# Interleaving two arrays: each DMA queue carries loads and stores in a fixed order

## The chip, the core and the metric

The kernel runs on one core of a Trainium2 chip. The core's compute engines work in an on-chip memory of 128 partitions, and DMA engines, 16 of them, move data between that memory and the chip's main memory (HBM). The metric is the device time of one execution in microseconds (us). Before the change the median of three runs is 314.26 us (314.11 to 314.35).

## The reference

The reference takes two float32 arrays x and y of shape 32 x 256 x 1024 and interleaves them along the last axis:

```python
def reference(x, y):
    batch, seq, dim = x.shape
    result = np.zeros((batch, seq, dim * 2), dtype=np.float32)
    result[..., 0::2] = x
    result[..., 1::2] = y
    return result.astype(np.float32)
```

Each input has 33.55 MB, the output 67.11 MB. Every byte is read once and written once, 134.22 MB in all, and nothing is computed: the output is x and y woven together element by element.

## The kernel before

**Tiles.** Each input is taken as one flat run and cut into n = 8 tiles of 128 partitions by W = 8192 values, 4 MiB each, 32 KiB to a partition. A tile of x and a tile of y make 8 MiB of output. In a tile, partition p holds 8192 neighbouring values of the flat input, so its output is 16384 neighbouring values; the output is handled in two halves of 8192 values a partition (h = 0 and 1), 4 MiB each.

**Buffers.** There are two buffers for x (`xt`), two for y (`yt`), used by even and odd tiles in turn, and two for the output (`ot`), where `ot[0]` always takes half 0 of a tile and `ot[1]` half 1.

**Weaving.** VectorE (DVE in the profile) does all of it, four copies a tile: for each half, one copy of 4096 values of x a partition into the even places of `ot[h]` (L67), and one of y into the odd places (L70). Each copy counts up the semaphore `woven`, so that tile k has been woven when `woven` is 4k + 4. Before the first copy of a half VectorE waits until the tile's x has landed, and, from the second tile on, until the store that last read `ot[h]` has landed (`osem[h]`). Before the first y copy it waits for y.

**Who issues what.** DMAs are issued from two engines, SP (its queue is q1 in the profile) and ScalarE (ACT, queue q10). Each queue starts its transfers in the order of issue, and an engine that waits for a semaphore holds back everything behind it in its own program.

- SP issues the loads: the left half of x's first tile (L45), then all of y's first tile (L55), then for each tile x (L52) and y (L55). From the third tile on, x waits until the third copy of the tile two before (which frees that `xt`), and y until the fourth.
- ScalarE issues the right half of x's first tile (L46), and then all stores (L76): for each tile and half, wait until both copies of the half are done, then store. The very first store, half 0 of tile 0, is cut into a quarter (8 KiB a partition) and the rest (24 KiB).

So apart from the first half tile, one queue carries loads and the other stores. The first DMA of each of the two engines is moved ahead of the barrier that opens the program (in `tile_interleave_kernel`), so that it is issued at once.

**The end.** ScalarE waits for all stores of half 0 and clears the semaphores (L83); SP waits for all stores of half 1 (L84).

The functions that the change touches, and what calls them:

Of the kernel before, what the change touches and what calls it, by code (L numbers as in the profile page):

```python
# [3 lines left out]


def _interleave(nc, x, y, out):
    P = 128
    W = 8192
    H = W // 2  # L10

    total = 1
    for s in x.shape:
        total *= s
    n = total // (P * W)
    assert n * P * W == total
# [8 lines left out]
    ot = [nc.alloc_sbuf_tensor(f"ot{b}", [P, W], fp32).ap() for b in (0, 1)]  # L25

    xsem = [nc.alloc_semaphore(f"xsem{b}") for b in (0, 1)]
    hsem = nc.alloc_semaphore("hsem")
    ysem = [nc.alloc_semaphore(f"ysem{b}") for b in (0, 1)]
    woven = nc.alloc_semaphore("woven")  # L30
    osem = [nc.alloc_semaphore(f"osem{b}") for b in (0, 1)]
# [24 lines left out]

    for k in range(n):
        b = k % 2
        for h in (0, 1):
            c = slice(h * H, (h + 1) * H)  # L60
            if h == 0:
                nc.vector.wait_ge(xsem[b], 16 * (k // 2 + 1))
            elif k == 0:
                nc.vector.wait_ge(hsem, 16)
            if k:
                nc.vector.wait_ge(osem[h], stored(k, h))
            nc.vector.tensor_copy(out=ot[h][:, 0::2], in_=xt[b][:, c]).then_inc(woven, 1)  # L67
            if h == 0:
                nc.vector.wait_ge(ysem[b], 16 * (k // 2 + 1))
            nc.vector.tensor_copy(out=ot[h][:, 1::2], in_=yt[b][:, c]).then_inc(woven, 1)  # L70

    for k in range(n):
        for h in (0, 1):
            nc.scalar.wait_ge(woven, 4 * k + 2 * h + 2)
            for c in parts(k, h):
                nc.scalar.dma_start(  # L76
                    out=os_[k][:, h * W : (h + 1) * W][:, c], in_=ot[h][:, c]
                ).then_inc(osem[h], 16)

    nc.scalar.wait_ge(osem[0], stored(n, 0))  # L80
    used = sorted(s.num for s in [*xsem, hsem, *ysem, woven, osem[0]])
    assert used == list(range(used[0], used[-1] + 1)), used
    nc.scalar.sem_clear(range(used[0], used[-1] + 1))  # L83
    nc.sync.nop(nofuse=True).wait_op(osem[1], stored(n, 1), "sem-ge").then_inc(  # L84
        osem[1], -stored(n, 1)
    )


def kernel(tc, x, y, out):
    nc = tc.nc  # L90
    tc.close()
    tc.compile()

    _interleave(nc, x, y, out)

    blocks = nc.main_func.blocks
    for engine in (mybir.EngineType.SP, mybir.EngineType.Activation):
        opening = blocks[0].instructions
# [14 lines left out]
        opening.insert(gate, moved)  # L113
        at.instructions = body
        blocks[0].instructions = opening


# [1 line left out]
_INS = ['x', 'y']  # L119
_OUTS = [((32, 256, 2048), 'float32')]  # L120


# [23 lines left out]
```

## Time and profile before

| | |
|---|---|
| median of three runs | 314.26 us |
| profiled execution, device time | 314.21 us |
| its span (first to last instruction) | 312.9 us |
| moved through HBM | 67.11 MB read, 67.11 MB written, 429 GB/s over the span |
| VectorE busy | 71.9 us, 32 copies of 2.29 us |
| VectorE waiting for stores to free an output buffer | 206.3 us in 14 waits |
| 4 MiB loads of x, y, median from issue to landing | 24.4 us, 41.5 us |
| 4 MiB stores, median from issue to landing | 34.1 us |

How to read it: the span is what one profiled execution shows between its first and its last instruction; its device time is 1.3 us longer. The page gives the busy share of the DMA engines in 40 equal slices, where a 9 means 90% or more, and for each queue the number of packets, the megabytes and the time that they took as a share of 16 engines over the span. A packet is what one engine moves in one go: here one partition's row of a transfer, or the small one that reports its end. The waits list says which engine stood idle for what: total, number of times, longest. The view by windows gives, for chosen stretches of the span, what was busy and how many GB/s were moved.

### The profile page before, as it was taken

How to read it: one execution, taken by the hardware profiler on the slowest of the kernel's cores; microseconds unless marked ns; L12 is line 12 of the kernel's file. 1: busy time of each engine (PE TensorE's matmuls, PEld its weight loads, DVE VectorE, ACT ScalarE, POOL GpSimd, SP SyncE). 2: the span in 40 equal slices, each digit the busy share in tenths (PEclk: the TensorE clock that was granted, in tenths of full speed). 3: DMA queues.
4: the chain of work that ended last, by engine and by line, in shares of the span. 5: the costliest groups of instructions: out<-in, count | busy, mean ns of one | idle time of the engine just before them, and what ended most of it. 6: DMA issues, size and time to landing. Idle time of an engine off the chain costs nothing.

```text
span 312.9 us, 114 instructions
## 1 busy us (share of the span) xinstructions
DVE 71.9 (23%) x32; POOL 0.2 (0%) x4
## 2 busy tenths in 40 slices
DVE  0216000501305023050230503205032050415400
POOL 0000000000000000000000000000000000000000
DMA  8999999999999999999999999999999999999998
GB/s 344 461 406 431 436 402 431 440 465 406 448 423 431 440 406 465 402 469 402 469 402 465 406 457 415 436 436 419 452 402 469 402 469 402 469 402 461 411 444 360
DMA packets 4896, 134.22 MB, mean 429 GB/s; under 512 B 544, under 2 KB 544, under 8 KB 544
## 3 DMA queue, kind: packets, MB, share of 16 engines
q10 hardware_dynamic: 2592, 69.21, 51.3%
q1 hardware_dynamic: 2304, 65.01, 48.5%
HBM read 67.11 MB, written 67.11 MB: 429 GB/s over the span
## 4 chain that ended last, share of the span: by engine, by line
DMA 82%; DVE 12%; issue 0%
DMA out_dram<-ot 76%; DMA yt<-in_y_dram 7%; DVE ot L70 6%; DVE ot L67 6%
## 5 line engine op out<-in xcount | busy, mean ns | idle before, releaser
L67 DVE COPY ot<-xt 128x4096 f32<-128x4096 f32 x16 | 36.7, 2295 | 218.0 <-DMA out_dram<-ot 206.3
L70 DVE COPY ot<-yt 128x4096 f32<-128x4096 f32 x16 | 36.6, 2288 | 8.0 <-DMA yt<-in_y_dram 8.0
L130 POOL MEMSET const-uint8-127<- 128x1 uint8 x1 | 0.1, 102 | 0.0
L130 POOL MEMSET const-bfloat16-1.0<- 128x1 bf16 x1 | 0.1, 101 | 0.0
L130 POOL MEMSET const-float32-0.0<- 128x1 f32 x1 | 0.1, 98 | 0.2 <-issue 0.2
L130 POOL MEMSET const-float32-1.0<- 128x1 f32 x1 | 0.1, 98 | 0.0
## 6 DMA issues: line engine op xcount, KB each, us to landing
out_dram<-ot ACTq DMA_DIRECT2D x15, 4096.0 KB, 34.1
yt<-in_y_dram SPq DMA_DIRECT2D x8, 4096.0 KB, 41.5
xt<-in_x_dram SPq DMA_DIRECT2D x7, 4096.0 KB, 24.4
out_dram<-ot ACTq DMA_DIRECT2D x1, 3072.0 KB, 32.8
xt<-in_x_dram SPq DMA_DIRECT2D x1, 2048.0 KB, 11.7
xt<-in_x_dram ACTq DMA_DIRECT2D x1, 2048.0 KB, 13.4
out_dram<-ot ACTq DMA_DIRECT2D x1, 1024.0 KB, 16.1
```

Source lines behind the costliest of these rows:

```text
L67: nc.vector.tensor_copy(out=ot[h][:, 0::2], in_=xt[b][:, c]).then_inc(woven, 1)
L70: nc.vector.tensor_copy(out=ot[h][:, 1::2], in_=yt[b][:, c]).then_inc(woven, 1)
L130: nc = _bacc.Bacc("TRN2", target_bir_lowering=False, num_devices=1)
```

## The change

Both queues now carry loads and stores. SP has x and half 0 of the output, ScalarE has y and half 1. Each issues in a fixed order.

- At the start: SP loads the left halves of x's and y's first tiles, then x's second tile; ScalarE loads the right halves, then y's second tile. A new semaphore `gsem` reports y's right half.
- Then for each tile k: SP waits for the first two copies, stores half 0, waits for the third copy, and loads x of tile k + 2 into the buffer just freed. ScalarE waits for all four copies, stores half 1, and loads y of tile k + 2.
- The first store is no longer cut in two.
- The last tile is not woven into `ot`. Its half 0 goes into the `xt` buffer, and its half 1 into the `yt` buffer, that tile 6 has left free. VectorE waits for its own count `woven` to reach 28 before it writes there, and not for `osem`.
- The copies of VectorE, their order and their shapes stay as they are, apart from that destination. In the changed file the copies are lines L78 and L83, the stores L57 and the loads of tiles 2 to 7 L63.
- `osem` is allocated in another place, so that the range that ScalarE clears at the end is still one run of numbers.

```diff
-    Q = W // 4
+    def woven_in(k, h):
+        if k == n - 1:
+            return (xt if h == 0 else yt)[(k + 1) % 2]
+        return ot[h]
 
-    def parts(k, h):
-        return [slice(0, W)] if k or h else [slice(0, Q), slice(Q, W)]
+    lo, hi = slice(0, H), slice(H, W)
+    nc.sync.dma_start(out=xt[0][:, lo], in_=xs[0][:, lo]).then_inc(xsem[0], 16)
+    nc.scalar.dma_start(out=xt[0][:, hi], in_=xs[0][:, hi]).then_inc(hsem, 16)
+    nc.sync.dma_start(out=yt[0][:, lo], in_=ys[0][:, lo]).then_inc(ysem[0], 16)
+    nc.scalar.dma_start(out=yt[0][:, hi], in_=ys[0][:, hi]).then_inc(gsem, 16)
+    nc.sync.dma_start(out=xt[1], in_=xs[1]).then_inc(xsem[1], 16)
+    nc.scalar.dma_start(out=yt[1], in_=ys[1]).then_inc(ysem[1], 16)
 
-    def stored(k, h):
-        return 16 * sum(len(parts(j, h)) for j in range(k))
-
-    nc.sync.dma_start(out=xt[0][:, :H], in_=xs[0][:, :H]).then_inc(xsem[0], 16)
-    nc.scalar.dma_start(out=xt[0][:, H:], in_=xs[0][:, H:]).then_inc(hsem, 16)
     for k in range(n):
         b = k % 2
-        if k >= 2:
-            nc.sync.wait_ge(woven, 4 * (k - 2) + 3)
-        if k:
-            nc.sync.dma_start(out=xt[b], in_=xs[k]).then_inc(xsem[b], 16)
-        if k >= 2:
-            nc.sync.wait_ge(woven, 4 * (k - 2) + 4)
-        nc.sync.dma_start(out=yt[b], in_=ys[k]).then_inc(ysem[b], 16)
+        for h, (eng, t, src, sem) in enumerate(
+            ((nc.sync, xt, xs, xsem), (nc.scalar, yt, ys, ysem))
+        ):
+            eng.wait_ge(woven, 4 * k + 2 * h + 2)
+            eng.dma_start(
+                out=os_[k][:, h * W : (h + 1) * W], in_=woven_in(k, h)
+            ).then_inc(osem[h], 16)
+            if k + 2 < n:
+                if h == 0:
+                    eng.wait_ge(woven, 4 * k + 3)
+                eng.dma_start(out=t[b], in_=src[k + 2]).then_inc(sem[b], 16)
...
-            if k:
-                nc.vector.wait_ge(osem[h], stored(k, h))
-            nc.vector.tensor_copy(out=ot[h][:, 0::2], in_=xt[b][:, c]).then_inc(woven, 1)
+            if 0 < k < n - 1:
+                nc.vector.wait_ge(osem[h], 16 * k)
+            if k == n - 1 and h == 0:
+                nc.vector.wait_ge(woven, 4 * k)
+            dst = woven_in(k, h)
+            nc.vector.tensor_copy(out=dst[:, 0::2], in_=xt[b][:, c]).then_inc(woven, 1)
             if h == 0:
                 nc.vector.wait_ge(ysem[b], 16 * (k // 2 + 1))
-            nc.vector.tensor_copy(out=ot[h][:, 1::2], in_=yt[b][:, c]).then_inc(woven, 1)
+            elif k == 0:
+                nc.vector.wait_ge(gsem, 16)
+            nc.vector.tensor_copy(out=dst[:, 1::2], in_=yt[b][:, c]).then_inc(woven, 1)
 
-    for k in range(n):
-        for h in (0, 1):
-            nc.scalar.wait_ge(woven, 4 * k + 2 * h + 2)
-            for c in parts(k, h):
-                nc.scalar.dma_start(
-                    out=os_[k][:, h * W : (h + 1) * W][:, c], in_=ot[h][:, c]
-                ).then_inc(osem[h], 16)
...
-    nc.scalar.wait_ge(osem[0], stored(n, 0))
+    nc.scalar.wait_ge(osem[0], 16 * n)
```

More of the change, by code (lines that the diff above doesn't have):

```diff
@@ L25, in _interleave @@
     ot = [nc.alloc_sbuf_tensor(f"ot{b}", [P, W], fp32).ap() for b in (0, 1)]
+    osem = [nc.alloc_semaphore(f"osem{b}") for b in (1, 0)][::-1]
     xsem = [nc.alloc_semaphore(f"xsem{b}") for b in (0, 1)]
     hsem = nc.alloc_semaphore("hsem")
+    gsem = nc.alloc_semaphore("gsem")
     ysem = [nc.alloc_semaphore(f"ysem{b}") for b in (0, 1)]
     woven = nc.alloc_semaphore("woven")
-    osem = [nc.alloc_semaphore(f"osem{b}") for b in (0, 1)]
     xs = [rows(x, P * W, k) for k in range(n)]
@@ L64, in _interleave @@
                 nc.vector.wait_ge(hsem, 16)
[L65 to L67 removed]
+            if 0 < k < n - 1:
[4 more added lines that the diff above has]
+            nc.vector.tensor_copy(out=dst[:, 0::2], in_=xt[b][:, c]).then_inc(woven, 1)
             if h == 0:
                 nc.vector.wait_ge(ysem[b], 16 * (k // 2 + 1))
[L70 to L81 removed]
+            elif k == 0:
+                nc.vector.wait_ge(gsem, 16)
+            nc.vector.tensor_copy(out=dst[:, 1::2], in_=yt[b][:, c]).then_inc(woven, 1)
+    nc.scalar.wait_ge(osem[0], 16 * n)
+    used = sorted(s.num for s in [*xsem, hsem, gsem, *ysem, woven, osem[0]])
     assert used == list(range(used[0], used[-1] + 1)), used
     nc.scalar.sem_clear(range(used[0], used[-1] + 1))
[L84 to L85 removed]
+    nc.sync.nop(nofuse=True).wait_op(osem[1], 16 * n, "sem-ge").then_inc(
+        osem[1], -16 * n
     )
```

## The prediction, made before the changed kernel ran

> **What bounds the kernel now.** I read the page first: its two DMA lines and the queues.
>
> ```profile
> span 312.9 us, 114 instructions
> DVE 71.9 (23%) x32; POOL 0.2 (0%) x4
> DMA  8999999999999999999999999999999999999998
> DMA packets 4896, 134.22 MB, mean 429 GB/s; under 512 B 544, under 2 KB 544, under 8 KB 544
> q10 hardware_dynamic: 2592, 69.21, 51.3%
> q1 hardware_dynamic: 2304, 65.01, 48.5%
> ```
>
> The two queues (q1 is issued by SP, q10 by ScalarE) together occupy 16 DMA engines for 99.8% of the span, while VectorE is busy for 23%. The question is whether that busy time is full speed. The view by windows, cut where transfers land, answers it (window, its length, VectorE and POOL busy, clock, DMA share, GB/s):
>
> ```profile
> 2.00:22.00 20.00, 2.30 (x1) 0.00 (x0) 1.00 1.01 433
> ...
> 26.00:32.60 6.60, 2.72 (x2) 0.00 (x0) 1.00 0.98 392
> ...
> 193.07:231.80 38.73, 9.01 (x5) 0.00 (x0) 1.00 1.00 433
> ...
> 283.84:293.52 9.68, 4.50 (x3) 0.00 (x0) 1.00 1.00 433
> 293.52:303.20 9.68, 4.49 (x2) 0.00 (x0) 1.00 1.00 433
> ```
>
> The first row holds loads alone, first on two queues and then on one. The third is a whole tile in the steady part, loads on one queue and stores on the other. The last two hold stores alone, on one queue. All show 433 GB/s, so neither direction nor the number of queues moves the rate. One row stands out: 392 GB/s around the first stores.
>
> The trace's records of single packets say what the rate is made of. A 32 KiB packet (one partition's row) takes 1.213 us and the next on the same engine starts 1.210 us after it, load or store. 16 KiB steps take 0.607, 24 KiB 0.908, 8 KiB 0.305, and a completion packet 0.006. A 4 MiB transfer puts 8 rows on each engine: 8 x 1.210 + 0.006 = 9.69, and the trace has 9.68. I weighed every packet at these steps and compared the sum with the time that passed. From 1.38 us, when the first packet starts, only four stretches lose anything: 0.89 us up to 11.7 (the first 16 KiB packets take 1.0 to 1.5 instead of 0.61), 0.47 between 27.4 and 32.6 (loads beside the first 8 KiB stores take 1.25 to 1.59 instead of 1.213), 0.05 around 40 (the first 24 KiB stores) and 0.21 in the last 9.7 us (engines end 0.33 apart). The sum: 1.38 + 309.85 of packets + 1.62 lost = 312.85, against a span of 312.88.
>
> The waits show that VectorE is never late, and the timeline shows the end:
>
> ```profile
> DVE ot L67 <- DMA out_dram<-ot: 206.3, 14, 28.9
> ...
> 288.42 9.96 ACTq L76 DMA_DIRECT2D out_dram<-ot  x2
> 293.51 2.30 DVE L67 COPY ot<-xt 128x4096 f32<-128x4096 f32 x1 [5.12 <-DMA out_dram<-ot]
> ```
>
> VectorE waits 206.3 us for output buffers. The last store is issued at 298.0, while its predecessor runs until 303.2; there is no gap to close at the end. The chain of waits puts 82% on DMA and 12% on copies, but those copies lie beside other transfers: the windows around them still move 433 GB/s.
>
> The profiled execution took 314.21 us, 1.33 more than its span; the median of the three runs is 314.26.
>
> **The change, part by part.**
>
> *Packets.* Before: 4 MiB loads 7 of x and 8 of y, 15 such stores, two 2 MiB halves of x, and a first store cut into 1 and 3 MiB: 34 transfers. After: 14 loads and 16 stores of 4 MiB, four halves of 2 MiB: again 34. The first store becomes whole (1.210 instead of 0.305 + 0.908 a row: -0.02 for 8 rows), y's first tile becomes halves (2 x 0.607 instead of 1.210: +0.03). Sum 0.0. SP and ScalarE issue 17 each (before 16 and 18) at 0.33 to 0.48 us each on the issuing queue, always with earlier transfers still in the ring.
>
> *Order in the rings.* Each ring now holds load, store, load, store. If both have packets, they take turns row by row (the trace shows q1, q10, q1, q10 from 3.2 us on), so two 4 MiB transfers, one of each ring, take 2 x 9.68 = 19.36. Loads of tiles 0 and 1 (16.8 MB) end at 1.38 + 0.89 + 4 x 9.68 = 41.0; the stores of tile 0 end at 60.4, the loads of tile 2 at 79.7, the stores of tile 1 at 99.1, and so on: 38.72 a tile, as now. For most of the time both rings go in the same direction; the windows price that at 433 either way.
>
> *The waits.* A ring runs dry only if its next transfer comes late. Tile k's copies start when tile k-1's stores have landed; four copies take 2.30 + 3 x 2.21 = 8.9 us. SP's store of tile k is issued after two of them (4.5 us), its x load after three, ScalarE's store and y load after four. Meanwhile the rings hold the loads of tile k+1, 19.36 us of work. The cover left is 19.36 - 8.9 = 10.4 us for ScalarE and 14.9 for SP, so I cost these waits at nothing. Behind SP's wait for the store is queued its x load of tile k+2, which waits with it; it goes into the ring behind that store and is not wanted before the store has left it, 19.36 us later. If the cover were gone, up to 8.9 us a tile would show.
>
> *The last tile.* The loads of tile 7 land when tile 6's stores start. Woven into the freed xt and yt buffers, it needs no output buffer: 8.9 us of copies under 19.36 us of tile 6's stores. The added wait on VectorE's own count costs one copy's drain, under 0.1 us (2.29 busy against 2.21 from start to start), and is covered. Without the spare buffers, the copies would wait for tile 6's stores with nothing behind them: 4.5 us of idle rings.
>
> *The first stores.* This is the one term that the trace cannot price. They now follow loads in both rings, at 40 instead of 28 us, in 32 KiB rows. The loss was 0.47 beside 8 KiB rows; the nearest row in size (24 KiB) lost 0.05, but came after stores had been running. The bounds are 0 and 0.94 (both rings lose it); I take 0.25, between the two rows. That is 0.25 - 0.52 = -0.27.
>
> *The end.* Both rings now end near each other. ScalarE's clearing of semaphores (0.063 us at 303.2 before) can fall behind the last landing: 0 to +0.06; I take +0.03. The spread of the engines, 0.33, stays.
>
> *A rule that speaks against.* In the windows and packets, a load row that follows a store row on the same engine starts as promptly as any other, 1.210 us after it. The Trainium skill (HBM Reference, Latency) gives 0.2 us for an access to HBM on average and 2 us under high load; if each of the 7 turns from stores back to loads exposed one, an estimate by that page would be +1.4 to +14 us. By the rows the turns cost 0, and the trace does not agree for turns between two rings; turns inside a ring it does not show.
>
> The sum: 314.21 + 0.0 - 0.27 + 0.03 = 313.97, which I round to **314.0**.
>
> **The rivals.**
>
> *A. Every turn costs (slower).* In the changed kernel both rings turn from loads to stores and back. The rings turn 8 times to stores and 7 times to loads; before, the kernel had one such turn, at 27.4. If the 0.47 lost there is the price of starting stores after a stretch of loads, and not of the first stores alone, 7 more of them cost 3.3 us: 317.3. If turning back to loads costs as much as the start of the first loads (about 0.72 us of too long packets per engine), 7 x 0.72 = 5.0 comes on top: 322.3. At a tenth to a half of the first price it is 314.3 to 315.6. For it: the loss is real, and sits exactly at the first change of direction. Against it: in the steady part each engine changes direction at every row without losing anything, and at 277.8, where loads run out and only stores are left, no packet is late. It decides from 0.63 / 14 = 0.045 us a turn. Chance 0.24, most of it between 315.0 and 317.3.
>
> *B. The first loss goes and something of the edges with it (faster).* All that can go is 1.62 us; the start (0.89) and the spread (0.21) come from packets that the change leaves alone. Losing the whole 0.47 and 0.05 gives 314.21 - 0.52 = 313.7, still short of 0.2%. Only with a shorter start or end does it get to 313.4. Chance 0.17.
>
> *C. The change does not do what it says: a ring runs dry after all*, for example because one ring falls behind and a store is issued after its ring has emptied. The other ring then uses the engines alone at 433 GB/s (rows 283.84 and 293.52), so nothing is lost until both are empty, more than 10.4 us too late. At the last tile it would cost 4.5 us: 318.5. Chance 0.03.
>
> **How the numbers follow.** A measurement of this kernel can tell about 0.2% from no change, 0.63 us: 313.63 to 314.89. The forecast, no measurable change with the time between 313.65 and 314.85, has 0.56. Slower is A and C, 0.27; faster is B, 0.17. The forecast's own range is 313.7 to 314.7 (the bounds 0 and 0.94 of the first stores, with 0.06 at the end). The stated range, 313.5 to 316.0, takes in most of B and the cheaper half of A; outside it lie the dearer half of A (0.12), C (0.03) and about 0.04 of B.
>
> **What the profile of the changed kernel would show.** Right: both queues near 50%, and a DMA line of nines; windows of 19.36 us that hold loads only and then stores only, each at 433 GB/s; VectorE waiting about 30 us a tile for the output, and at tile 7 for the loads of x instead, near 272 us; the last store of each ring issued more than 10 us before its ring runs empty; a tile every 38.72 us. Wrong for the waits: slices under 9 in the DMA line, or both rings idle. A would show as a tile period above 38.72 with packets longer than 1.213 us at each turn, and as windows under 433 GB/s around it. The first stores are right if the stretch around 41 us loses less than 0.47. The prediction fails if a turn inside a ring has a price that turns between rings do not have.

## The result, and the profile after

The changed kernel takes 317.39 us (median of five runs, 316.78 to 317.93), the kernel before 314.22 us (five runs, 314.11 to 314.35). The ratio is 1.0102, with a 95% interval of 1.0087 to 1.0117: 3.2 us slower. The prediction was 314.0, between 313.5 and 316.0. The profiled execution took 317.93 us, with a span of 316.6 (before 314.21 and 312.9). In five of the kernels below single runs lie more than 1.5% above the kernel's fastest; the ratios leave those out, and a median that holds them is marked with a star.

The page of the changed kernel, its first lines:

```profile
span 316.6 us, 114 instructions
...
DVE 71.4 (23%) x32; POOL 0.2 (0%) x4
...
DMA  8999999999999999999999999999999999999995
...
DMA packets 4896, 134.22 MB, mean 424 GB/s; under 512 B 544, under 2 KB 544, under 8 KB 544
...
q10 hardware_dynamic: 2448, 67.11, 49.6%
q1 hardware_dynamic: 2448, 67.11, 49.3%
```

The packets and bytes are the same as before, evenly split now. The DMA line has its nines as before: no slice shows empty queues. Only its last digit fell, from 8 to 5. Yet the span is 3.7 us longer, so the engines were busy for longer with the same bytes, and at the end some of them had nothing left to do. The view by windows (window, its length, VectorE and POOL busy, clock, DMA share, GB/s) shows both:

```profile
2.00:22.00 20.00, 2.60 (x2) 0.00 (x0) 1.00 1.01 433
36.32:46.00 9.68, 0.00 (x0) 0.00 (x0) 1.00 0.95 383
43.00:60.00 17.00, 0.00 (x0) 0.00 (x0) 1.00 1.00 434
82.00:99.00 17.00, 0.00 (x0) 0.00 (x0) 1.00 1.00 434
178.54:217.69 39.15, 8.91 (x5) 0.00 (x0) 1.00 1.00 431
283.84:293.52 9.68, 1.95 (x1) 0.00 (x0) 1.00 1.00 433
293.52:303.20 9.68, 0.00 (x0) 0.00 (x0) 1.00 1.00 433
312.90:316.60 3.70, 0.00 (x0) 0.00 (x0) 1.00 0.15 62
```

Stretches that only load (2 to 22) or only store (43 to 60, 82 to 99, and the two from 283.84 to 303.20) move 433 or 434 GB/s, as priced. Around the first turn from loads to stores it is 383. (A window counts a row whole where it starts, so the rate of a short window is rough; what a turn costs is read from the single rows below.) A whole tile (from 178.54) moves 431, where before it was 433. And the last row is the new thing: from 312.9 us on, where the kernel before had ended, 3.7 us go by at 62 GB/s, since few of the 16 engines are still at work.

The waits and the timeline show the same lateness from VectorE's side (start, duration, instruction, idle time before it and what ended that):

```profile
DVE ot L78 <- DMA out_dram<-ot: 183.9, 6, 32.3
```

```profile
60.69 2.29 DVE L78 COPY ot<-xt 128x4096 f32<-128x4096 f32 x1 [32.30 <-DMA out_dram<-ot]
...
99.90 2.29 DVE L78 COPY ot<-xt 128x4096 f32<-128x4096 f32 x1 [30.30 <-DMA out_dram<-ot]
...
178.54 2.29 DVE L78 COPY ot<-xt 128x4096 f32<-128x4096 f32 x1 [30.39 <-DMA out_dram<-ot]
...
217.69 2.29 DVE L78 COPY ot<-xt 128x4096 f32<-128x4096 f32 x1 [30.24 <-DMA out_dram<-ot]
...
276.32 2.29 DVE L78 COPY xt<-xt 128x4096 f32<-128x4096 f32 x1 [10.60 <-DMA xt<-in_x_dram]
...
281.41 0.34 SPq L57 DMA_DIRECT2D out_dram<-xt  x1
...
285.82 0.35 ACTq L57 DMA_DIRECT2D out_dram<-yt  x1
```

The first copies of tiles 1, 2, 4 and 5 start 39.2 us apart (39.21 from the first to the second, 39.15 from the third to the fourth), not 38.72. VectorE waits some 30 us a tile for the stores, so it holds nothing up: the transfers are late.

**Where in the packets.** As in the prediction I weighed every packet at its nominal time (32 KiB: 1.213 us), and call what a packet takes beyond it its loss. The records do not name the engine; each packet was linked to the one that ends where it starts, which gives 16 chains. A turn is the place where an engine goes from its last load row to its first store row or back. Times of rows and ends of engines, here and in the experiments, are set some 0.37 us later than the packet records have them, so that the last row ends with the span; the windows use the records' own times. A ring is what a queue has waiting on an engine. In the changed kernel the two rings turn at nearly the same time: SP's loads of tile 1 end at 40.4 us and ScalarE's at 43.4, then SP's end at 79.8 and ScalarE's at 82.7, and so on, about two rows apart on each engine.

```
loss per turn from loads to stores, us
at                41    79   118   157   196   235   274
mean of engines 0.61  0.28  0.12  0.12  0.16  0.09  0.15
last engine     0.54  0.41  0.45  0.63  0.62  0.42  0.56
turns from stores to loads: about 0.02, mean of engines

engines' ends: 12 from 312.9 to 313.8, then 315.6, 315.7, 315.7, 316.6
before:        16 from 312.55 to 312.88
```

At 41 us all engines lose, and at 79 nearly all. Later, most lose almost nothing, and the four that are behind lose 0.2 to 0.7 each time, nearly always on one of their last load rows in ScalarE's queue. At 197 us the twelve engines that start their last load row but one between 194.3 and 195.0 lose 0.00 to 0.14 at this turn, and the four that start it from 195.5 to 196.4 lose 0.49 to 0.71. The first engines start to store at 196.7; the rows that come late are load rows of the lagging engines that are under way then. The last engine's rows there: a load of x at 195.2 on time, a load of y at 196.4 that takes 0.62 too long, x's completion at 198.2, y's last load row on time, the first store row at 199.5 on time. Lateness breeds lateness: the engines spread from 0.3 to 3.7 us (below: they drift), and a transfer has landed only when the last engine is done: VectorE's copy at 276.32 began as the last engine finished the load of x's tile 7 at 276.3.

So the 3.7 us of span are: the engines' mean end 1.24 later (313.92 against 312.68), and the last engine 2.5 us further from that mean (2.69 against 0.20). Of the 1.24, the table's first line (sum 1.53) less what the first stores cost before (0.47 and 0.05) explains 1.0; 0.2 is not assigned.

### The profile page after: what moved, and what is told of

The parts are those of the page before. It is cut to its first block, busy times and chain, and to the rows that moved or that the text cites. A ratio compares the mean times of both kernels' runs of the same rounds, so it can differ in the third digit from the quotient of the medians.

```text
span 316.6 us, 114 instructions
## 1 busy us (share of the span) xinstructions
DVE 71.4 (23%) x32; POOL 0.2 (0%) x4
## 2 busy tenths in 40 slices
DMA packets 4896, 134.22 MB, mean 424 GB/s; under 512 B 544, under 2 KB 544, under 8 KB 544
## 4 chain that ended last, share of the span: by engine, by line
DMA 73%; DVE 14%; another core or an unknown queue 3%; issue 0%; DVEq 0%
DMA out_dram<-ot 66%; DMA yt<-in_y_dram 6%; DVE ot L83 6%; DVE ot L78 5%; DVE xt L83 1%; DVE xt L78 1%; DVE yt L83 1%; DVE yt L78 1%; DVEq L74 0%; DVEq L76 0%
## 5 line engine op out<-in xcount | busy, mean ns | idle before, releaser
L78 DVE COPY ot<-xt 128x4096 f32<-128x4096 f32 x14 | 32.1, 2291 | 195.8 <-DMA out_dram<-ot 183.9
L83 DVE COPY ot<-yt 128x4096 f32<-128x4096 f32 x14 | 32.0, 2289 | 7.5 <-DMA yt<-in_y_dram 7.5
L78 DVE COPY xt<-xt 128x4096 f32<-128x4096 f32 x1 | 2.3, 2295 | 10.6 <-DMA xt<-in_x_dram 10.6
L83 DVE COPY xt<-yt 128x4096 f32<-128x4096 f32 x1 | 2.3, 2295 | 0.5 <-DMA yt<-in_y_dram 0.5
L83 DVE COPY yt<-yt 128x4096 f32<-128x4096 f32 x1 | 2.3, 2289 | 0.0
L78 DVE COPY yt<-xt 128x4096 f32<-128x4096 f32 x1 | 2.3, 2286 | 0.0
```

Source lines behind the costliest of these rows:

```text
L78: nc.vector.tensor_copy(out=dst[:, 0::2], in_=xt[b][:, c]).then_inc(woven, 1)
L83: nc.vector.tensor_copy(out=dst[:, 1::2], in_=yt[b][:, c]).then_inc(woven, 1)
```

## The experiments

Ratios are to the kernel before, run beside them on the same chip (its medians: 314.22 to 314.28). Diffs are against the changed kernel.

### One part alone: queue roles undone

```diff
...
-            eng.wait_ge(woven, 4 * k + 2 * h + 2)
-            eng.dma_start(
+            nc.scalar.wait_ge(woven, 4 * k + 2 * h + 2)
+            nc.scalar.dma_start(
...
-                if h == 0:
-                    eng.wait_ge(woven, 4 * k + 3)
-                eng.dma_start(out=t[b], in_=src[k + 2]).then_inc(sem[b], 16)
+                nc.sync.wait_ge(woven, 4 * k + 3 + h)
+                nc.sync.dma_start(out=t[b], in_=src[k + 2]).then_inc(sem[b], 16)
```

> The changed kernel with one part undone: SP issues all loads of whole tiles and ScalarE all stores again; the halves at the start, the uncut first store and the last tile woven into freed buffers stay. If the order in the rings costs the 3.2 us (either theory of turns), this takes 313.8 to 314.4, and no packet between 45 and 300 us is longer than 1.22 us. If the last tile or the start costs it, it stays at 316.8 to 317.9. The first stores are whole here: if the loss of 0.47 us beside them came from the 8 KiB rows, it is below 0.1 now; if it came from stores that begin beside loads, 0.3 or more is left.

Measured: 314.66 us (10 runs), ratio 1.0015 (1.0006 to 1.0025), a quarter of a microsecond above the range expected of the queues' order. Here the stores begin earlier, near 27 us; the first window holds this turn, the others are those of the changed kernel:

```profile
24.00:31.00 7.00, 4.25 (x2) 0.00 (x0) 1.00 0.99 384
...
36.32:46.00 9.68, 0.00 (x0) 0.00 (x0) 1.00 1.00 433
...
313.00:317.00 4.00, 0.00 (x0) 0.00 (x0) 1.00 0.00 0
```

This kernel too is slower around its first stores, 384 GB/s, but after them no row loses more than 0.01 us until the end, and none starts after 313.0 us. The order of the queues costs 2.7 of the 3.2 us. The rest of the change, that is y in halves, the uncut first store and the last tile in xt and yt, costs the other 0.4: the first stores lose 0.73 (before 0.47), and the engines end 0.62 apart (before 0.33). With 32 KiB rows the first loss is larger and not smaller, so it did not come from the 8 KiB rows alone.

### Is it a price for each turn?

Each 4 MiB transfer as two halves by column, stores and loads in alternation, so that there are nearly twice as many turns (13 to stores in each ring; the changed kernel has 7):

```diff
...
+            for c in (lo, hi):
+                eng.dma_start(
+                    out=os_[k][:, h * W : (h + 1) * W][:, c], in_=woven_in(k, h)[:, c]
+                ).then_inc(osem[h], 16)
+                if k + 2 < n:
+                    if h == 0 and c is hi:
+                        eng.wait_ge(woven, 4 * k + 3)
+                    eng.dma_start(out=t[b][:, c], in_=src[k + 2][:, c]).then_inc(sem[b], 16)
```

> The changed kernel with each 4 MiB load and store from tile 2 (loads) and tile 0 (stores) on cut into two halves of 2 MiB and interleaved: store half, load half, store half, load half, both rings in step. Twice as many turns from loads to stores (15 instead of 8), each after half as long a stretch of loads, with rows of 16 KiB. The shorter rows by themselves cost 8 x 0.004 a transfer, about 0.9 us in all, and the added completion packets 0.2. Theory that each turn has a price: about 3 us more than the changed kernel beyond that, 320 to 322. Theory that the price grows with the length of the stretch: no more than the 1.1 us, 317.5 to 319.

Measured: 316.13 us* (4 runs), ratio 1.0057 (1.004 to 1.0073). Neither expectation holds: nearly twice the turns, and faster than the changed kernel. One of the four runs took 323.71 us; it left no trace.

```profile
36.32:46.00 9.68, 0.00 (x0) 0.00 (x0) 1.00 0.95 372
46.00:55.68 9.68, 0.00 (x0) 0.00 (x0) 1.00 1.00 430
```

The first turn loses 0.84 in the mean (first row). At the turns at 51, 61, 71 and 80 us one row loses 0.11 and no other more than 0.03, the engines end 0.6 apart, and the 430 of the second row comes from 16 KiB rows (0.607 for half of 1.210) and more completions. So in the run that left a trace turns have no fixed price, and the first one is a case by itself.

The same transfers in halves, but both stores first and then both loads, as long a stretch as in the changed kernel:

```diff
...
+            for c in (lo, hi):
+                eng.dma_start(
+                    out=os_[k][:, h * W : (h + 1) * W][:, c], in_=woven_in(k, h)[:, c]
+                ).then_inc(osem[h], 16)
...
+                for c in (lo, hi):
+                    eng.dma_start(out=t[b][:, c], in_=src[k + 2][:, c]).then_inc(sem[b], 16)
```

> The changed kernel with each load and store of whole tiles cut into a left and a right half of 2 MiB, issued one behind the other, so that the order of directions, the turns and the length of each stretch stay those of the changed kernel, and only the rows are 16 KiB instead of 32. The shorter rows and added completion packets cost 1.1 us by themselves, on top of about 314.6 for a kernel with these parts and no loss at turns: 315.7. Theory that the length of the stretch of loads sets the loss: the turns cost what they do in the changed kernel, 318 to 319.5, engines 2.5 us or more apart at the end. Theory that the row length sets it (a row in flight at the turn is what is delayed, and an engine that lags by a row is hit): 315.5 to 316.5, engines within 1 us.

Measured: 318.11 us (4 runs), ratio 1.0108 (1.0081 to 1.0135). The slow time comes back with 16 KiB rows, within the range expected if the length of the stretch matters, so it was not the short row that made the kernel with twice the turns faster. The losses lie elsewhere, though: 0.9 at the first turn, nothing at 79, 118 and 157 us, 0.61 on all engines at 195, then 0.06 twice. The engines end 2.5 apart.

I also halved by partitions, to have short stretches with 32 KiB rows:

```diff
...
+            for c in (slice(0, P // 2), slice(P // 2, P)):
+                eng.dma_start(
+                    out=os_[k][c, h * W : (h + 1) * W], in_=woven_in(k, h)[c]
+                ).then_inc(osem[h], 16)
...
```

> The kernel with twice as many turns once more (store half, load half, store half, load half), but the halves are partitions 0 to 63 and 64 to 127 instead of left and right, so the rows keep their 32 KiB. Theory of the row length: the losses at later turns are back and the engines drift apart, 316.5 to 319, with 2 us or more between the first and the last engine's end. Theory of the stretch: as in the kernel with 16 KiB rows there is no loss after the first turn, 314.8 to 315.5, engines within 1 us.

Measured: 524.2 us (4 runs), ratio 1.6686 (1.6605 to 1.6768): a miss by every theory, and no answer to this question.

```profile
42.00:61.00 19.00, 0.00 (x0) 0.00 (x0) 1.00 1.04 238
100.00:200.00 100.00, 13.07 (x6) 0.00 (x0) 1.00 1.00 252
```

The DMA share is full, at 238 to 252 GB/s: all engines busy, with 32 KiB packets of twice the time, while both queues work in the same 64 partitions.

### Does one engine alone lose at a turn?

Transfers of 17 rows, six tiles, nothing woven:

```diff
+    R, T = 17, 6
...
-    nc.sync.dma_start(out=xt[1], in_=xs[1]).then_inc(xsem[1], 16)
+    nc.sync.dma_start(out=xt[1][:R], in_=xs[1][:R]).then_inc(xsem[1], 16)
...
```

> A measurement by itself, most of the work left out: transfers of 17 rows of 32 KiB, in which one DMA engine should carry all rows, both rings in step, six loads and six stores a ring in the order load, load, store, load, store and so on; the stores write a constant that VectorE sets, and the output is not the interleaved one. If the loss at a turn belongs to the single engine, the last load row before each first store row takes 1.3 to 2.0 us, as in the changed kernel (five turns, 0.1 to 0.9 us each). If it needs 16 engines that turn at once and meet in HBM, every row takes 1.213 us.

```profile
DMA packets 432, 13.37 MB, mean 27 GB/s; under 512 B 24, under 2 KB 24, under 8 KB 24
```

Measured (one run): 27 GB/s is 1/16 of 433, one engine. One load row took 1.841 us, at the first turn (83.2 us); no other row took more than 1.274. So in this run the first turn costs one engine 0.63 by itself, and later turns cost it nothing, though its two rings turn at the same time: the later losses seem to need other engines.

### Does a ring have to change direction?

SP loads and ScalarE stores, but made to take turns, by splitting transfers 3/4 and 1/4 and waiting for the first part:

```diff
...
+        nc.scalar.wait_ge(woven, 4 * k + 2)
+        if k + 1 < n:
+            nc.scalar.wait_ge(psem[1 - b], 16 * (k // 2 + 1))
+        nc.scalar.dma_start(out=os_[k][:, :W], in_=woven_in(k, 0)).then_inc(osem[0], 16)
...
+            nc.sync.wait_ge(woven, 4 * k + 4)
+            nc.sync.wait_ge(tsem, 16 * (k + 1))
+            nc.sync.dma_start(out=xt[b], in_=xs[k + 2]).then_inc(xsem[b], 16)
...
```

> Loads on SP's queue and stores on ScalarE's, but made to take turns: a tile's stores are issued when three quarters of the next tile's y have landed (2.4 us before that stretch of loads ends), and the next loads when three quarters of the second store have landed. So all 16 engines go load, store, load, store in stretches of 19.4 us as in the changed kernel, with no ring that changes its direction. Theory that the stretches cost it (stores that begin again after a pause delay the load rows in flight): 0.1 to 0.6 us a turn and engines drifting 2 us or more apart, 316 to 319. Theory that it needs rings that change direction: one loss at the first stores and none later, engines within 0.8 us, 314.5 to 315.5.

Measured: 318.36 us (4 runs), ratio 1.0135 (1.0121 to 1.0149).

```profile
56.00:65.68 9.68, 4.47 (x2) 0.00 (x0) 1.00 1.02 417
...
95.00:104.68 9.68, 4.56 (x3) 0.00 (x0) 1.00 1.00 407
```

Every 39 us (61, 100, 140, 179, 218, 258) the mean engine loses 0.38 to 0.60 on load rows, though each ring keeps its direction. Their sum, 2.9 us, is the larger part of the 4.6 by which its profiled span exceeds that of the kernel with roles undone (317.8 against 313.3). But the loss lies at the turns from stores to loads, on the first load rows, where the changed kernel lost 0.02. The turns from loads to stores are free here, the first one too: 0.05 from 36 to 48 us, 0.00 at 80, 0.01 at 119. At each of these the engine's first store row follows its own last load row, the engines being within 0.8 us of each other. So a turn can cost without any ring changing its direction, but this run, whose time alone fits the theory of turning engines, doesn't show the changed kernel's loss.

### Loads drained before stores

Each store waits until the next tile's loads have landed, so that no load is in flight beside the first stores:

```diff
+            if k + 1 < n:
+                eng.wait_ge(xsem[1 - b], 16 * ((k + 1) // 2 + 1))
+                eng.wait_ge(ysem[1 - b], 16 * ((k + 1) // 2 + 1))
```

> The changed kernel in which both queues, before each store, wait until x and y of the next tile have landed. So no load is in flight on any engine when stores begin, and engines that lag are waited for at every tile. Each of seven turns costs the time to fill empty rings, 1.4 to 3 us: 324 to 336 in all. Theory that the losses hit loads in flight on engines that lag: no packet over 1.3 us after the first stores and all engines within 0.8 us at the end. Rival, that an engine loses at the turn whatever is in flight: the spread at the end is 2 us or more as before.

Measured: 332.91 us (2 runs), ratio 1.0592 (1.0572 to 1.0611).

```profile
55.00:64.68 9.68, 1.18 (x1) 0.00 (x0) 1.00 0.96 379
75.04:84.72 9.68, 0.00 (x0) 0.00 (x0) 1.00 0.78 335
84.72:94.40 9.68, 0.00 (x0) 0.00 (x0) 1.00 1.01 433
```

Between the turns the rate is 433 again (third row). Part of the theory held: with no load in flight when the stores begin, no load row is late there (0.10 at the first stores, where the changed kernel lost 0.61), and the engines, which now wait for one another at every turn, end within 0.14 us. Part failed. The turn to stores (second row) costs some 2 us of empty rings, and the turn to loads (first row), free in the changed kernel, costs 0.67 to 0.75 on every engine, on the last store rows. Draining is no cure.

### Is it the engines being apart?

A load of 17 rows of 4 KiB puts one engine behind by a little, once, in the changed kernel and in the one with queue roles undone:

```diff
+    nc.scalar.dma_start(out=spare, in_=xs[0][:17, :1024]).then_inc(esem, 16)
```

> The changed kernel with one small load more at the start, 17 rows of 4 KiB that should all fall to one DMA engine, so that this engine is about 2.6 us behind the others from then on. Theory that lagging engines are hit again at every turn: this engine loses 0.4 us or more at each of the 8 turns and ends 5 to 8 us after the first engine, 319 to 321. Rival, that certain engines lose whatever their lag: it ends 2.6 us later than it would have, 317 to 319.5, and its losses at the turns are no larger than those of the others.

> The same small load added to the kernel whose queues carry loads alone and stores alone. Here no stretch ends and begins again, so under every theory the engine stays about 2.6 us behind and does not lose more: 316.5 to 317.5.

Measured: 324.67 us (2 runs; ratio 1.0332, 1.0311 to 1.0353) and 321.35 us (2 runs; ratio 1.0226, 1.0206 to 1.0247). In the first, 14 engines end between 317.0 and 317.2, one at 318.3, and the handicapped one at 323.09: followed row by row it loses 6.9 us from 62 us on, and its lag at the start has become 6 us, as the theory of late engines says. The second is a miss. There each ring has one direction, and still load rows lose, 0.1 to 0.8 us in the mean in every 19.4 us from 85 to 271 us and up to 1.15 a row, and the engines' ends spread from 315.3 to 319.9. So "it happens only where rings turn" is wrong.

The small load did more than make one engine late, though. Its 17 rows took turns with SP's rows, so on that engine SP's transfers moved ahead (in the second kernel SP's load of y's tile 1 ends there at 44.2 us, on the others at 56.2), and later the transfers of the other engines moved too: from 88 us on the two rings' transfers end 2 to 4 us apart on most engines, where with the queue roles undone alone they end 8 to 11 apart. Whether it is the lateness or this distance that costs, the second run can't tell.

### What sets it off: the distance between the rings?

In the changed kernel the two rings turn two rows apart and in the same direction. Where the queues have fixed roles and nothing delays them, their transfers end 7 to 12 us apart. The first attempt gave half of x's second tile to ScalarE, so that SP should be a whole transfer ahead and the rings run in opposite directions:

```diff
-    nc.sync.dma_start(out=xt[1], in_=xs[1]).then_inc(xsem[1], 16)
+    cut = 4096
+    nc.sync.dma_start(out=xt[1][:, :cut], in_=xs[1][:, :cut]).then_inc(xsem[1], 16)
+    nc.scalar.dma_start(out=xt[1][:, cut:], in_=xs[1][:, cut:]).then_inc(isem, 16)
```

> The changed kernel with one edit: tile 1 of x is loaded half by SP and half by ScalarE, so that SP's ring is one whole 4 MiB transfer ahead of ScalarE's. Each ring still goes load, store, load, store with as many turns, but one ring loads while the other stores. Theory of phases (the loss comes where both rings have loaded for a while and stores begin): back to 313.8 to 314.5, engines end within 0.5 us of one another. Theory of the ring's turn (a ring that goes from loads to stores loses, whatever the other ring does): 316.8 to 317.9 as before, and engines 3 us or more apart at the end.

Measured: 323.56 us (4 runs), ratio 1.0322 (1.028 to 1.0363). The rings did run in opposite directions, and it is far slower. Their transfers end 2.4 us apart again (50.7 and 53.1).

```profile
310.00:313.00 3.00, 0.00 (x0) 0.00 (x0) 1.00 0.81 350
313.00:317.00 4.00, 0.00 (x0) 0.00 (x0) 1.00 0.69 295
317.00:323.00 6.00, 0.00 (x0) 0.00 (x0) 1.00 0.06 27
```

14 engines end at 316.1 to 316.2 and two at 320.8 and 322.1: the last six microseconds move 27 GB/s.

Three more cuts were to move the distance in steps, `cut` at 7168, 6144 and 5120:

> The changed kernel with the last 1024 of 8192 columns of x's tile 1 loaded by ScalarE instead of SP (SP's ring 1 MiB ahead). The rings' transfers then end 7.3 and 12.1 us from one another instead of 2.4 and 16.9. Theory that what costs is two rings turning within two rows of each other: no loss after the first stores, engines within 0.9 us, 314.4 to 315.2. Rival, that rings or stretches that turn cost it wherever the other ring is: 316.5 to 318.

> The same with 2048 columns (2 MiB ahead): transfers end 12.1 and 7.3 us apart. Rings turning near each other: no loss after the first stores, 314.4 to 315.2. Turns anywhere: 316.5 to 318. Stretches of loads alone are halved, 9.7 us, with stores that begin beside loads in flight, so a theory that stores beginning beside loads cost it expects 0.3 us or more at each of 7 starts, 316.5 or more.

> The same with 3072 columns (3 MiB ahead): transfers end 16.9 and 2.4 us apart, so that the rings turn close to each other again, in opposite directions and with the other ring first. Rings turning near each other: losses and drift are back, 316 to 324, as with a whole transfer's lead (323.6). Rival, that the share of time in one direction matters: it lies between the kernels with 2 MiB and 4 MiB and gets no cheaper from 1 to 4.

Measured: 327.55 us* (ratio 1.0343, 1.0283 to 1.0403), 326.28 us* (ratio 1.0242, 1.0195 to 1.0288) and 326.26 us* (one of four runs at 317.43, no interval). They missed their purpose. The rings take turns row by row, whatever the length of the row, so a shorter row shifts nothing: the transfers end at 50.7 and 53.1 us in all three. They count as repeats of the kernel with the whole lead, and they show how far the same order scatters, from 317.4 to 331.5, while the kernel before stays within 314.1 and 314.6 on that chip.

So the distance has to be moved in rows. A small load on ScalarE's queue gives each engine 8 rows (or 4) of 512 bytes there, while SP's ring goes on with rows of the tile; 8 rows first, 4 rows first, or 8 first and 4 behind the half tile (shown):

```diff
+    nc.scalar.dma_start(out=spare[:128], in_=xs[0][:128, :128]).then_inc(esem, 16)
     nc.scalar.dma_start(out=xt[0][:, hi], in_=xs[0][:, hi]).then_inc(hsem, 16)
+    nc.scalar.dma_start(out=more, in_=xs[0][:64, 128:256]).then_inc(fsem, 16)
```

> The changed kernel with one tiny load (128 rows of 512 bytes of x into a spare buffer) first on ScalarE's queue, in the place where the kernel with the early write had its write. Since the rings take turns row by row, its 8 rows on each engine put SP's ring ahead and the rings' transfers should end near 9.7 us apart. Theory that the distance of the rings' turns decides: no loss after the first stores, engines within 0.9 us, 314.7 to 315.3, as with the early write (315.0). Rival, that the early write took the loss away: losses at every turn and drift as in the changed kernel, 316.5 to 318.5.

> The same with 64 rows of 512 bytes, 4 on each engine: about half the shift, transfers of the two rings end 5 to 7 us apart. Theory of the distance: still no loss after the first stores, 314.7 to 315.5, if four rows or more are enough; 316 to 318 if the distance has to be half a transfer. Rival as above: 316.5 to 318.5.

> The kernel with 8 tiny rows once more, and a second tiny load (64 rows of 512 bytes, 4 on each engine) behind the right half of x's first tile on ScalarE's queue. In the kernel with 8 tiny rows, the two rings' transfers ended 2.4 us apart; four rows more should put them 7 to 12 us apart, with nothing written early. Theory that the distance of the rings' turns decides: no loss after the first stores, engines within 1 us, 314.7 to 315.5, as with the early write. Rival, that the early write took the loss away: losses at the turns and drift, 317 to 328.

Measured: 8 rows 327.5 us (4 runs; ratio 1.0442, 1.0409 to 1.0475), 4 rows 321.44 us (4 runs; ratio 1.0243, 1.0204 to 1.0283), 12 rows 314.95 us* (10 runs; ratio 1.0022, 1.0012 to 1.0032). With 8 rows the transfers end 2.0 to 2.4 us apart (50.8 and 53.2); the engines end 6.0 apart. With 4 rows they end at the same time (51.7 and 51.7); rows lose 0.7 in the mean at each of 90, 130 and 208 us, and the engines end 3.9 apart. With 12 rows they end 4.9 us apart at first (59.2 and 64.1) and 8.0 to 8.5 later, and behind the first stores (0.5) only one row loses anything worth the name, 0.5 at 97. One of its ten runs took 328.25 us; it left no trace, so whether the engines drifted in it is not known. The timeline of the run with a trace, at the same copy of three tiles in a row, and the window of its end:

```profile
154.87 2.30 DVE L84 COPY ot<-xt 128x4096 f32<-128x4096 f32 x1 [17.08 <-DMA out_dram<-ot]
...
193.60 2.30 DVE L84 COPY ot<-xt 128x4096 f32<-128x4096 f32 x1 [17.10 <-DMA out_dram<-ot]
...
232.35 2.30 DVE L84 COPY ot<-xt 128x4096 f32<-128x4096 f32 x1 [17.09 <-DMA out_dram<-ot]
```

```profile
313.00:317.00 4.00, 0.00 (x0) 0.00 (x0) 1.00 0.00 0
```

The tiles are 38.73 and 38.75 us apart, against 38.72 in the prediction, and no row starts after 313.0, where in the changed kernel the last engines work on to 316.6. Both rings still carry loads and stores in the order of the change.

### An early write

Another idea was that the engines have to get used to writing HBM: a store of 64 KiB, from HBM to HBM, first on ScalarE's queue, in the changed kernel and in the one before:

```diff
+    nc.scalar.dma_start(out=os_[0][:, W : W + 128], in_=xs[0][:, :128]).then_inc(wsem, 16)
```

> The changed kernel with one tiny write to HBM first on ScalarE's queue (128 rows of 512 bytes, copied from x, later overwritten by the real store). Theory that the first writes of an execution cost something once and set the engines apart, and that this spread grows at later turns: the loss of 0.6 us around 41 us is gone, the engines stay within 1 us and the time is 314 to 315.5. Rival, that the turns cost what they do without it: 316.8 to 318.5.

> The kernel before with the same tiny early write. Theory that first writes cost once: the loss of 0.47 us around 30 us is gone, and the time is 313.6 to 314.1, which is faster than both kernels. Rival, that loads alone followed by stores cost it: 314.2 to 314.6, with load rows of 1.3 to 1.6 us still around 30 us.

Measured: 315.01 us (10 runs; ratio 1.0019, 1.0006 to 1.0033) and 314.48 us (11 runs; ratio 1.0001, 0.999 to 1.0012). The changed kernel lost its drift, as hoped, but not its first loss: that came at the first stores all the same, 1.0 in the mean. The kernel before kept its first loss too (0.4) and gained nothing.

```profile
24.00:31.00 7.00, 0.41 (x1) 0.00 (x0) 1.00 1.03 375
...
62.00:71.68 9.68, 0.00 (x0) 0.00 (x0) 1.00 1.00 433
```

The first row shows that loss, the second a stretch with SP's next turn from loads to stores, at 66.8, at 433. And the early write had moved the rings: their transfers end 9.7 us apart (66.8 and 76.5). The kernel with 12 rows, which writes nothing early, gets the same time; so the write is not needed; what both kernels have in common is the shift.

### What the runs say together

```
kernel                 rings' transfers   both rings    loss at      engines'  time
                       end apart, us      load for, us  later turns  spread
changed                2.4                17            yes          3.7       317.39
16 KiB rows            1.2                18            at some      2.5       318.11
whole lead             2.4                2.4           yes          6.0       323.56
shift of 8 rows        2.0 to 2.4         2.4           yes          6.0       327.5
shift of 4 rows        0.0                0             yes          3.9       321.44
twice the turns        1.2, then 3.5-6.2  8.5, 3.5      no           0.6       316.13
shift of 12 rows       4.9, then 8.5      14.5, 11      one row      0.9       314.95
early write            9.7                9.7           no           0.5       315.01
handicap, fixed roles  1.7-3.6 from 88    never         yes          4.7       321.35
handicap, changed      9.5, then 7.3-2.5  9.5, then 4.8 yes          6.1       324.67
queue roles undone     8.2 to 11.2        never         no           0.6       314.66
before                 7.3 to 12.1        never         no           0.3       314.22
```

Neither the direction in which the rings run nor the length for which both load sorts this table. The distance between the rings does, nearly: five orders that drift have it at 2.4 us or less, and the kernel with fixed roles and a handicapped engine, which drifts though no ring of it turns, has 1.7 to 3.6 on most engines from 88 us on. Of the kernels that are further apart, only the other one with a handicapped engine drifts. That is a rule for these orders, not a mechanism. Four things stand against more. With twice the turns the rings were 1.2 us apart from 51 to 81 us, and with 16 KiB rows until 157 us, and hardly a row was late. In the changed order with a handicapped engine, rows are late from 136 us on while the rings' transfers still end 9.5 us apart. Where draining or fixed roles bring all engines to the turn together, the turns to stores are free and those to loads are not. And the rule rests on one trace of each kernel: one run with twice the turns took 8 us longer than the others, and one with 12 rows 13 us. The kernel before, too, had two of 21 runs above 316 us on one chip.

One rival is not tested. Each of these kernels ran on one chip, and the 8 and 4 rows on another chip than the 12 rows, so chips that differ in how far an order drifts are not ruled out there. On the chip that ran the whole lead, the queue roles undone and twice the turns, the first took 323.4 us or more in every run, the second 315.0 or less. What delays the late rows inside the chip stays open. No kernel beat the one before; the best in the new order (314.95) is still 0.2% behind.

## Why the prediction was wrong

**Packets: right.** 4896 packets and 134.22 MB, evenly split, and 17 transfers on each ring.

**Order in the rings: the step that failed.** "For most of the time both rings go in the same direction; the windows price that at 433 either way." The windows do: 434 GB/s within the stretches. But they price stretches, and I took the price of the turn between two stretches, which inside one ring no row of before shows, from rows that are no such turns: the row-by-row alternation of the steady part, and 277.8, where loads ran out while stores had long been running. Measured, the turns from loads to stores cost the mean engine 1.5 us in all, of which the first is 0.6, and the engines' drift, which the prediction had no term for, 2.5. The tile came out at 39.2 us instead of 38.72. A transfer has landed with the last of its 16 engines, and in "The spread of the engines, 0.33, stays", in the step on the end, lay the largest single error: it became 3.7. The count was off as well: each ring turns 7 times to stores and 6 times to loads, not 8 and 7.

The prediction named as its sign of failing a price of turns inside a ring. That is half of it: with the roles undone the later losses went, but load rows were late as well in two kernels in which no ring turns (318.36 and 321.35 us).

**The waits: right.** The DMA line stays at nines, and VectorE waits 30 us a tile, as said. The cover of 10.4 and 14.9 us was never used up.

**The last tile: right in its place, late in time.** VectorE waited for x there (10.6 us) and not for the output, at 276.3 and not near 272; the last stores were issued at 281.4 and 285.8, 14.6 and 12.7 us before their rings were through with tile 6's stores, so more than the 10 us that were given as the sign.

**The first stores: mis-sized.** Taken at 0.25 between the bounds 0 and 0.94. The first turn lost 0.61 in the changed kernel and 0.73 with the roles undone. The row of 24 KiB (0.05), to which I leaned, came after stores had been running; the runs show that first stores which begin beside loads in flight cost 0.4 to 1.1 once.

**The start and the end.** The windows have the first packets between 0.9 and 1.1 us, so the 1.38 of the prediction is 0.38 too late, and these 0.38 lie behind the last packet; the sum is the same. The +0.03 by ScalarE's clearing cannot be told beside a last engine 2.8 us behind the twelfth.

**The price of an access.** The turns from stores back to loads lost 0.02 in the changed kernel; the loss sits on the other side, at the last loads before the stores. In the kernel with fixed roles and alternating stretches the first load rows behind the stores lost 0.4 to 0.6 in the mean, and in the drained order the turns to loads cost 0.7, but on the store rows before them. The Trainium skill (HBM Reference, Latency) gives 0.2 us for an access to HBM on average and 2 us under high load. The estimate made from it, one such access exposed at each turn, does not agree with the changed kernel; the 0.4 to 0.6 lie between its two figures, which does not show that they are such an access.

**The rivals.** A's number, 317.3, is nearly the time measured, and its sign was right, but it got there by seven more equal prices of 0.47 on all engines (with the right count six, 317.0). Its signs came: a tile period above 38.72, rows over 1.213 at the turns, windows under 433. The first turn (0.61) is such a price; the other six together cost the mean engine 0.92, and in the trace of the kernel with twice the turns the later ones cost next to nothing. The rest is drift. Its chance of 0.24 was too low for a reason that I could have seen: I wrote that it decides from 0.045 us a turn, a tenth of the one turn that the trace showed, and that the trace does not show turns inside a ring; a price that no row shows, with a bound of 0.47, deserved half of its size, not zero. B did not come about: nothing of the first loss went. C did not either; both rings had packets until the end.

## What to carry to other kernels

An average rate over a long window prices a stretch, not the seam between stretches; where a change multiplies seams, price them by the only seam that the trace has, however rare it was. A transfer ends with its slowest engine, so look at the spread of the engines' ends (the last digits of the DMA line show it) as well as at the mean. Where two queues must both carry loads and stores, keep the ends of their transfers several rows apart, and see in a trace that the distance is really there; one direction for each queue was safe here only as long as nothing brought their transfers together.

## What was not expected of the hardware

- **A small lag can grow.** One engine that was given 17 rows of 4 KiB more, which also moved its two rings against each other, ended 6 us behind the others (323.09 against 317.0 to 317.2). In the kernel with the whole lead, the late rows take up to twice their time (1.21 us more than 1.213).
- **Rings alternate row by row, whatever the row.** With rows of 20 to 28 KiB in one ring against others in the other, the transfers' ends moved by less than 0.1 us. The Trainium skill (DMA: Bandwidth & Descriptors, Queues, rings and completion order) has an engine drain some 9 to 17 descriptors of a queue before it switches; these traces show a switch after every row.
- **64 partitions at a time are half as fast.** With both queues in the same half of the partitions, 238 to 252 GB/s instead of 433. The Trainium skill (DMA: Bandwidth & Descriptors, The descriptor swizzle) assigns partitions 0 to 63 to one half of the ports and the others to the other half; half of the ports would make a factor of two, an estimate by that page; the run shows 1.7 to 1.8.
- **First stores beside loads cost once.** 0.4 to 1.1 us in the mean, on load rows, in every kernel with 128-partition transfers where loads are in flight when the first stores begin, even behind an early write; 0.63 in the run on a single engine. Where no load is in flight then, 0.05 and 0.10.
